# One layer of a hybrid network on one core: where the second doubled block of weights stands, and how a norm's scale reaches all partitions

## The chip, the cores and the metric

The kernel runs on one core of one Trainium2 chip. The metric is the device time of one launch in microseconds (us); lower is better. Three runs of the kernel before gave 2309.09 us in the median (2308.48 to 2310.07).

## The reference

One layer works on 256 tokens of 2048 features, all in fp32:

```python
h = h + 0.5 * swiglu(rmsnorm(h, ffn1_norm), ffn1_w_in, ffn1_w_out)          # 2048 -> 2 x 5632 -> 2048
h = h + hybrid_mixer(rmsnorm(h, mix_norm), ...)                             # 2048 -> 11296, 4096 -> 2048
h = h + 0.5 * swiglu(rmsnorm(h, ffn2_norm), ffn2_w_in, ffn2_w_out)
gate = sigmoid(rmsnorm(h, ple_norm) @ ple_w_gate)
h = h + gate * (p @ ple_w_proj)
return rmsnorm(h, final_norm)
# rmsnorm(x, w) = x * rsqrt(mean(x * x, features) + 1e-6) * w
```

The mixer holds a short gated convolution, a state-space part over two chunks of 128 tokens and 32 heads (each product with its own decay mask), and a norm over four groups of 512 features. So a token's mean square over 2048 features is wanted five times and over 512 features four times: nine norms.

## The kernel before

Features lie on the 128 partitions, tokens along the free axis: `h` is 128 x 16 x 256. Every large product is a `Gemm` object. It takes 256 output columns (two halves `j` of 128, a PSUM bank each) and walks the depth in chunks of four 128-row tiles. For each chunk SyncE loads 512 KB of weights (`w`, four buffers), ScalarE rounds them to `hi` (line 99) and VectorE makes `lo = w - hi` (line 100); `hi` and `lo` have three buffers each. The input is likewise held as a high part (columns 0 to 255) and a low part (256 to 511). Each depth tile then costs a pair of products: H (`hi` against 512 columns) and L (`lo` against the 256 high columns). Line 136 issues both. The results are added when the gemm ends (`gather`: ScalarE line 150, VectorE line 152).

In a chunk and half the four pairs stand as HLHLHLHL, or as HHLLHHLL, which I call a double block. Which ones do is set by `doubles`, line 120: the number is `k0 % 16 // 2 + j`, from 0 to 7 over four chunks with two halves each. The default (0, 4) gives two double blocks in every 32 pairs, twelve ordinary pairs apart; in the two feed-forward parts (`ffn`) only one number is given, so 24 to 32 ordinary pairs lie between.

A norm (class `Norm`) sums squares per partition into `nacc` (128 x 256). `sums` multiplies it, once per 128 tokens, as the stationary operand with one column of ones (line 194), so that the sums of 256 tokens stand on partitions as 128 x 2. VectorE scales and adds epsilon (line 211), GpSimd takes the power -0.5 of these two columns (line 213). `spread` brings this back to all partitions, with two products against the identity (line 221) and a copy to SBUF (line 224). Eight norms go this way; the last one has a variant for the end of the kernel. As a norm's factor multiplies the result of the product that follows, `sums` is called one gemm ahead of `spread`, and that gemm runs meanwhile.

The engines get their instructions from a scheduling layer that fixes an order for each engine; every engine works its queue strictly in that order. The weights' `hi` and `lo` have a raised priority (line 98).

Of the kernel before, what the change touches and what calls it, by code (L numbers as in the profile page):

```python
# [8 lines left out]
F32 = mybir.dt.float32  # L9
F32R = mybir.dt.float32r  # L10
AF = mybir.ActivationFunctionType
ALU = mybir.AluOpType
PSUM = bass.MemoryType.PSUM

P = 128
T = 256
D = 2048
KD = D // P
# [5 lines left out]
NCH = 2  # L24
EPS = 1e-6
KC = 4
# [19 lines left out]
S_ALL = S_CB + 24  # L46


@with_exitstack
def block_kernel(ctx, tc, xT, pT, small, dtp, w1, o1, wm, wdt, om, w2, o2, wg, wp, out):  # L50
    nc = tc.nc
    cst = ctx.enter_context(tc.tile_pool(name="cst", bufs=1))
# [3 lines left out]
    ev = ctx.enter_context(tc.tile_pool(name="ev", bufs=2))  # L56
    tmp = ctx.enter_context(tc.tile_pool(name="tmp", bufs=1))
# [5 lines left out]
    def aux(name):  # L63
        return aux_p.tile([P, 512], F32, tag="aux", name=name)
# [21 lines left out]
    V.tensor_scalar(out=mneg, in0=stri, scalar1=NEG, scalar2=None, op0=ALU.mult)  # L86
    pick = cst.tile([2 * HEADS, HEADS], F32R, name="pick")
    V.tensor_tensor(out=pick, in0=ident[0:2 * HEADS, 0:HEADS], in1=ident[0:2 * HEADS, HEADS:2 * HEADS], op=ALU.add)
    half = cst.tile([P, 2], F32, name="half")
    G.memset(half, -0.5)  # L90


    def parts(src, nk, cols):
# [10 lines left out]
    class Gemm:  # L104
# [2 lines left out]

        def __init__(self, src, K, rhs, cols=256, one=False, acc=None, doubles=(0, 4)):  # L110
            self.src, self.K, self.rhs, self.cols, self.one, self.doubles = src, K, rhs, cols, one, doubles
            self.acc = acc_p.tile([P, 2, 512], F32, tag="acc", name="acc") if acc is None else None
            self.banks = [self.acc[:, j, :] for j in range(2)] if acc is None else acc

        def chunk(self, k0, k1):
            hi, lo = parts(self.src[:, k0:k1, :], k1 - k0, self.cols)
            for j in range(self.cols // P):
                js = slice(j * P, (j + 1) * P)
                order = "HL" * (k1 - k0)
                if k1 - k0 == KC and k0 % 16 // 2 + j in self.doubles:  # L120
                    order = "HHLLHHLL"
                todo, acc, nh, nl = [], self.banks[j], k0, k0
                for part in order:
                    if part == "H":
                        k, w, nh = nh, hi, nh + 1
                    else:
                        k, w, nl = nl, lo, nl + 1
                    x, a = self.rhs(k), w[:, k - k0, js]
                    if self.one:
                        todo += [(acc[:, 0:T], a, x[:, i:i + T]) for i in ((0, T) if part == "H" else (0,))]  # L130
                    elif part == "H":
                        todo.append((acc, a, x))
                    else:
                        todo.append((acc[:, T:], a, x[:, 0:T]))
                for n, (o, a, b) in enumerate(todo):
                    nc.tensor.matmul(o, lhsT=a, rhs=b, start=(k0 == 0 and n == 0),  # L136
                                     stop=(k1 == self.K and n == len(todo) - 1))
# [6 lines left out]
    def gemm(*args, **kw):  # L144
        return Gemm(*args, **kw).all()
# [28 lines left out]
    class Norm:  # L174
# [24 lines left out]
            self.total(self.acc, self.ps, True, False)  # L199

        def sums(self):
            v = tmp.tile([P, 2], F32, tag="nv", name="nv", bufs=2)
            if self.more is None:
                ps = aux("nps")
                self.total(self.acc, [ps[:, c:c + 1] for c in range(NCH)], True, True)
                src = [(v, ps[:, 0:2])]
            else:
                self.total(self.more[:, 0, :], self.ps, False, True)
                src = [(v[:, c:c + 1], self.ps[c]) for c in range(NCH)]
            for o, i in src:  # L210
                V.tensor_scalar(out=o, in0=i, scalar1=1.0 / self.n, scalar2=EPS, op0=ALU.mult, op1=ALU.add)
            rt = tmp.tile([P, 2], F32, tag="nrt", name="nrt", bufs=2)
            G.tensor_tensor(out=rt, in0=v, in1=half, op=ALU.pow)  # L213
            self.rt = rt

        def spread(self, both=False):
            rt = self.rt
            pbs = [aux("npb") for _ in range(2 if both else 1)]
            for pb in pbs:
                for c in range(NCH):  # L220
                    nc.tensor.matmul(pb[:, c * P:(c + 1) * P], lhsT=rt[:, c:c + 1].to_broadcast([P, P]),  # L221
                                     rhs=ident, start=True, stop=True)
            r = tmp.tile([P, T], F32, tag=self.tag, name="r", bufs=2)
            (A.copy if both else V.tensor_copy)(out=r, in_=pbs[-1][:, 0:T])
            return (pbs[0], r) if both else r

        def finish(self, both=False):
            self.sums()
            return self.spread(both)

    def next_x(src, m, x, wcol, norm):

# [6 lines left out]
    def ffn(wi, wo, x, norm, wcol_next, begun=()):  # L239
        xn, nn, r = None, Norm(D, "rn"), None  # L240
        f0 = 0
        for third, nf in enumerate((15, 15, 14)):
            ga = blk.tile([P, 8, 512], F32R, tag="blk", name="ga")
            gb = blk.tile([P, 8, 512], F32R, tag="blk", name="gb")
            gx = lambda k: (ga if k < 8 else gb)[:, k % 8, :]
            held = []
            for f in range(nf):
                acc = begun[f].acc if f0 + f < len(begun) else gemm(wi[f0 + f], KD, x, doubles=(f % 2,))
                held.append((f, gather(acc)))
                if r is None and f == 0:  # L250
                    if not begun:
                        norm.sums()
                    continue
                if r is None:
                    r = norm.spread()
                for i, s in held:
                    V.tensor_tensor(out=s, in0=s, in1=bc2(r), op=ALU.mult)
                    sg = ev.tile([P, T], F32, tag="t1", bufs=5, name="sg")
                    A.activation(out=sg, in_=s[:, 0, :], func=AF.Silu)
                    V.tensor_tensor(out=sg, in0=sg, in1=s[:, 1, :], op=ALU.mult)  # L260
                    split(gx(i), sg)
                held = []
            if third == 2:
                xn = new_x()
            for m in range(0, KD, 2):
                acc = gemm(wo[m // 2][:, f0:f0 + nf, :], nf, gx, doubles=(0,))
                s = gather(acc, scale=0.5)
                hm = h[:, m:m + 2, :]
                V.tensor_tensor(out=hm, in0=s, in1=hm, op=ALU.add)
                if third == 2:  # L270
                    next_x(hm, m, xn, wcol_next, nn)
            f0 += nf
        return xn, nn
# [272 lines left out]
    for m in range(0, KD, 2):  # L546
        tail = m == KD - 2
        pr = proj(m) if tail else None
        for q in range(2 if tail else 1):
# [22 lines left out]
            for i in range(m + q, m + q + n):  # L572
                if i < POOL:
                    A.activation(out=hw[:, i, :], in_=h[:, i, :], func=AF.Copy,
                                 scale=sm[:, S_NF + i:S_NF + i + 1])
    pb, rf = nf.finish(both=True)
    for i in range(POOL):
        G.tensor_tensor(out=hw[:, i, :], in0=hw[:, i, :], in1=rf, op=ALU.mult)
        if i in (1, POOL - 1):
# [70 lines left out]
```

## Time and profile before

| | |
|---|---|
| median of three runs | 2309.09 us |
| the profiled execution | 2308.93 us, span 2307.2 us |
| TensorE busy | 2289.1 us (99%), 13308 products |
| VectorE, ScalarE busy | 1510.6 us (65%), 1140.1 us (49%) |
| GpSimd busy | 11.8 us (1%), 25 instructions |
| granted TensorE clock | 0.998 of full speed in the mean |

TensorE is busy in nearly all slices of the span, but matmuls overlap in the trace, so that "busy" doesn't say how dense they stand. The distance from one start to the next does, and it is what the rows below show.

### The profile page before, as it was taken

What the parts mean: (1) busy time and instruction counts of PE and PEld (TensorE: products, weight loads), DVE (VectorE), ACT (ScalarE), POOL (GpSimd) and SP (SyncE); (2) the same over time, 40 slices, a digit from 0 to 9 for tenths busy, and PEclk for the clock granted to TensorE, in tenths of its full rate; (3) what the DMA queues carried; (4) which work ended last, traced back from release to release, by engine and by line L of the source; (5) the groups of instructions that cost most, each with busy time, mean ns of one, the idle gap of its engine ahead of it and who ended that gap; (6) DMA issues with size and microseconds to landing.
All of it is one profiled execution on the core that took longest, in us unless ns stands there. A gap on an engine that the chain in (4) does not pass through costs nothing.

```text
span 2307.2 us, 33578 instructions
## 1 busy us (share of the span) xinstructions
PE 2289.1 (99%) x13308; PEld 1995.2 (86%) x13308; DVE 1510.6 (65%) x1936; ACT 1140.1 (49%) x1499; POOL 11.8 (1%) x25
## 2 busy tenths in 40 slices
PE   8999999999999999999999999999999999999997
PEld 7888888888888888888888888888888888888887
DVE  7665566656667777777777655566656665666776
ACT  6444444444455555444455444444444444444564
POOL 0000000000000000000000000000000000000000
PEclk9999999999999999999999999999999999999999
DMA  7666666665666655555555666666666666666654
GB/s 240 190 189 184 195 191 189 186 193 190 191 183 194 187 186 183 164 164 173 172 175 182 180 190 184 186 189 191 189 191 189 190 190 187 192 190 183 193 183 143
DMA packets 126862, 429.38 MB, mean 186 GB/s; under 512 B 13616, under 2 KB 20016, under 8 KB 126704
## 3 DMA queue, kind: packets, MB, share of 16 engines
q1 hardware_dynamic: 126144, 426.17, 61.1%
q8 instruction: 104, 1.70, 0.3%
q10 hardware_dynamic: 480, 0.80, 0.1%
q14 instruction: 54, 0.44, 0.0%
q0 software_dynamic: 80, 0.26, 0.0%
HBM read 425.08 MB, written 2.10 MB: 185 GB/s over the span
## 4 chain that ended last, share of the span: by engine, by line
PE 99%; DVE 0%; DMA 0%; ACT 0%; POOL 0%; issue 0%; DVEq 0%; POOLq 0%; ACTq 0%
PE acc L136 97%; PE pr L136 0%; PE yp L417 0%; PE ab L398 0%; PE npb L221 0%; DVE h L583 0%; DMA sm<-in_small 0%; PE yp L420 0%; PE xt L373 0%; PE st L387 0%; PE nps L194 0%; PE cb L366 0%; DVE xa L163 0%; POOL nrt L213 0%; PE dtT L432 0%
## 5 line engine op out<-in xcount | busy, mean ns | idle before, releaser
L100 DVE TENSOR_TENSOR lo<-w,hi 128x1024 fp32r<-128x1024 f32 (+1 forms) x834 | 990.6, 1188 | 703.6 <-ACT hi L99 690.2
L99 ACT CAST hi<-w 128x1024 fp32r<-128x1024 f32 (+1 forms) x834 | 850.9, 1020 | 1019.5 <-PE acc L136 835.2
L136 PE MATMUL acc<-xb,hi 128*128 128x512 f32 (+1 forms) x2264 | 782.1, 393 | 0.0
L136 PE MATMUL acc<-xa,hi 128*128 128x512 f32 (+1 forms) x2264 | 774.4, 395 | 6.1 <-DVE xa L163 6.1
L136 PE MATMUL acc<-xb,lo 128*128 128x256 f32 x2248 | 606.6, 278 | 0.0
L136 PE MATMUL acc<-xa,lo 128*128 128x256 f32 x2248 | 580.7, 279 | 0.0
L136 PEld LDWEIGHTS acc<-xb,hi 128*128 128x128 f32 x2264 | 415.7, 188 | 89.1 <-issue 0.7
L136 PEld LDWEIGHTS acc<-xa,hi 128*128 128x128 f32 x2264 | 405.0, 188 | 80.1 <-ACT hi L99 6.1
L136 PEld LDWEIGHTS acc<-xa,lo 128*128 128x128 f32 x2248 | 423.3, 188 | 25.7 <-DVE lo L100 0.7
L136 PEld LDWEIGHTS acc<-xb,lo 128*128 128x128 f32 x2248 | 422.2, 188 | 10.2 <-issue 0.5
L136 PE MATMUL acc<-ga,hi 128*128 128x512 f32 x768 | 262.3, 394 | 0.0
L136 PE MATMUL acc<-gb,hi 128*128 128x512 f32 x640 | 224.2, 394 | 0.0
L136 PE MATMUL acc<-ga,lo 128*128 128x256 f32 x768 | 197.3, 277 | 0.0
L136 PE MATMUL acc<-gb,lo 128*128 128x256 f32 x640 | 177.3, 277 | 0.0
L136 PEld LDWEIGHTS acc<-ga,hi 128*128 128x128 f32 x768 | 137.2, 188 | 25.1
L136 PEld LDWEIGHTS acc<-ga,lo 128*128 128x128 f32 x768 | 144.2, 188 | 8.5
L136 PEld LDWEIGHTS acc<-gb,hi 128*128 128x128 f32 x640 | 120.0, 188 | 27.9
L152 DVE SCALAR_TENSOR_TENSOR esum<-acc,elo 128x512 f32<-128x512 f32 (+1 forms) x196 | 133.6, 681 | 0.0
L136 PEld LDWEIGHTS acc<-gb,lo 128*128 128x128 f32 x640 | 120.1, 188 | 0.0
L150 ACT ACTIVATE elo<-acc 128x512 f32<-128x512 f32 (+1 forms) x196 | 116.1, 592 | 0.0
L136 PE MATMUL acc<-yb,hi 128*128 128x512 f32 x256 | 88.4, 398 | 0.0
L136 PE MATMUL acc<-ya,hi 128*128 128x512 f32 x256 | 88.3, 398 | 0.0
(144 smaller groups left out, 1108.9 us busy)
## 6 DMA issues: line engine op xcount, KB each, us to landing
w<-in_w SPq DMA_DIRECT2D x350, 512.0 KB, 4.5
w<-in_wm SPq DMA_DIRECT2D x176, 512.0 KB, 3.8
w<-in_o SPq DMA_DIRECT2D x144, 512.0 KB, 3.7
w<-in_om SPq DMA_DIRECT2D x64, 512.0 KB, 3.6
w<-in_wg SPq DMA_DIRECT2D x28, 512.0 KB, 4.5
w<-in_o SPq DMA_DIRECT2D x32, 384.0 KB, 3.7
w<-in_o SPq DMA_DIRECT2D x16, 256.0 KB, 3.4
w<-in_wp SPq DMA_DIRECT2D x8, 256.0 KB, 2.6
```

The lines of the kernel that those rows point to most:

```text
L99: A.copy(out=hi[:, :nk, :cols], in_=w[:, :nk, :cols])
L100: V.tensor_tensor(out=lo[:, :nk, :cols], in0=w[:, :nk, :cols], in1=hi[:, :nk, :cols].bitcast(F32), op=ALU.subtract)
L136: nc.tensor.matmul(o, lhsT=a, rhs=b, start=(k0 == 0 and n == 0), stop=(k1 == self.K and n == len(todo) - 1))
L150: A.mul(out=lo[:, :n, :], in_=acc[:, :n, T:], mul=scale)
L152: V.scalar_tensor_tensor(out=s[:, :n, :], in0=acc[:, :n, 0:T], scalar=scale, in1=lo[:, :n, :], op0=ALU.mult, op1=ALU.add)
```

## The change

Two things. The double blocks: `doubles` becomes `orders`, a table from the same number to an order. Number 0 keeps HHLLHHLL; number 1 ends in a double half and number 2 begins with one, so that the second block of four doubled pairs lies over the border of two halves and begins two ordinary pairs behind the first block, and 22 ordinary pairs follow. The feed-forward calls name one number as before and keep their order.

The norms: a matrix filled with 1/n is the stationary operand of one product whose moving operand is `nacc` (256 columns). Its result is the mean on every partition. VectorE adds epsilon over 256 columns, GpSimd takes the power over 256 columns into `r`, and the two products against the identity and the copy are gone. The last norm keeps its way.

```diff
+TWICE = {0: "HHLLHHLL", 1: "HLHLHHLL", 2: "HHLLHLHL"}
...
-    half = cst.tile([P, 2], F32, name="half")
+    half = cst.tile([P, T], F32, name="half")
     G.memset(half, -0.5)
+    mean = {}
+    for w in (D, 512):
+        mean[w] = cst.tile([P, P], F32, name=f"mean{w}")
+        G.memset(mean[w], 1.0 / w)
...
-                if k1 - k0 == KC and k0 % 16 // 2 + j in self.doubles:
-                    order = "HHLLHHLL"
+                if k1 - k0 == KC:
+                    order = self.orders.get(k0 % 16 // 2 + j, order)
...
         def sums(self):
...
+            ps = aux("nps")
+            nc.tensor.matmul(ps[:, 0:T], lhsT=mean[self.n], rhs=self.acc, start=True, stop=True)
+            v = ev.tile([P, T], F32, tag="t1", bufs=5, name="nv")
+            V.tensor_scalar(out=v, in0=ps[:, 0:T], scalar1=EPS, scalar2=None, op0=ALU.add)
+            self.r = tmp.tile([P, T], F32, tag=self.tag, name="r", bufs=2)
+            G.tensor_tensor(out=self.r, in0=v, in1=half, op=ALU.pow)
+
+        def spread(self):
+            return self.r
...
-                acc = begun[f].acc if f0 + f < len(begun) else gemm(wi[f0 + f], KD, x, doubles=(f % 2,))
+                acc = begun[f].acc if f0 + f < len(begun) else gemm(wi[f0 + f], KD, x, orders={f % 2: TWICE[0]})
...
-                acc = gemm(wo[m // 2][:, f0:f0 + nf, :], nf, gx, doubles=(0,))
+                acc = gemm(wo[m // 2][:, f0:f0 + nf, :], nf, gx, orders={0: TWICE[0]})
...
-    pb, rf = nf.finish(both=True)
+    pb, rf = nf.last()
```

TensorE at the first group norm of the mixer. Before, the two column sums, then one double block and ordinary pairs:

```order
L194 MATMUL nps<-ones,nacc 128x1 x2
L136 MATMUL acc<-xa,hi 128x512 x2
L136 MATMUL acc<-xa,lo 128x256 x2
L136 MATMUL acc<-xa,hi 128x512 x2
L136 MATMUL acc<-xa,lo 128x256 x2
L136 MATMUL acc<-xa,hi 128x512
L136 MATMUL acc<-xa,lo 128x256
L136 MATMUL acc<-xa,hi 128x512
L136 MATMUL acc<-xa,lo 128x256
```

Now, at the same place (`mean_106` is the matrix of 1/512):

```order
L211 MATMUL nps<-nacc,mean_106 128x256
L143 MATMUL acc<-xa,hi 128x512 x2
L143 MATMUL acc<-xa,lo 128x256 x2
L143 MATMUL acc<-xa,hi 128x512 x2
L143 MATMUL acc<-xa,lo 128x256 x2
L143 MATMUL acc<-xa,hi 128x512
L143 MATMUL acc<-xa,lo 128x256
L143 MATMUL acc<-xa,hi 128x512
L143 MATMUL acc<-xa,lo 128x256
L143 MATMUL acc<-xa,hi 128x512 x2
L143 MATMUL acc<-xa,lo 128x256 x2
L143 MATMUL acc<-xa,hi 128x512 x2
```

One product stands in place of two, and the second double block has come up from twelve pairs behind the first to two.

VectorE behind the same norm's line 211. Before (`nv` is the row ahead of these), the copy of `r` and the products with it (`yn`) stand some ten instructions on, one gemm later:

```order
L100 TENSOR_TENSOR lo<-w,hi 128x1024
L152 SCALAR_TENSOR_TENSOR esum<-acc,elo 128x512
L502 TENSOR_TENSOR esum<-esum,r 128x512
L100 TENSOR_TENSOR lo<-w,hi 128x1024
L504 TENSOR_TENSOR XT<-XT,esum 128x512
L100 TENSOR_TENSOR lo<-w,hi 128x1024
L187 TENSOR_TENSOR nacc<-sq 128x256
L100 TENSOR_TENSOR lo<-w,hi 128x1024
L224 COPY r<-npb 128x256
L100 TENSOR_TENSOR lo<-w,hi 128x1024
L152 SCALAR_TENSOR_TENSOR esum<-acc,elo 128x512
L487 SCALAR_TENSOR_TENSOR yn<-XT,sm,r 128x256 x4
```

Now:

```order
L213 TENSOR_SCALAR nv<-nps 128x256
L107 TENSOR_TENSOR lo<-w,hi 128x1024
L159 SCALAR_TENSOR_TENSOR esum<-acc,elo 128x512
L494 SCALAR_TENSOR_TENSOR yn<-XT,sm,r 128x256
L509 TENSOR_TENSOR esum<-esum,r 128x512
L494 SCALAR_TENSOR_TENSOR yn<-XT,sm,r 128x256
L107 TENSOR_TENSOR lo<-w,hi 128x1024
L511 TENSOR_TENSOR XT<-XT,esum 128x512
```

The first user of GpSimd's power (`yn`) has moved up to the third place behind `nv`, with one `lo` and one `esum` between; the next `lo` now stands behind it. (The `r` of line 509 is an older one.)

## Rows read from the trace of the kernel before

**Rows 1.** The page, part 4: the chain that ended last, by engine.

```profile
PE 99%; DVE 0%; DMA 0%; ACT 0%; POOL 0%; issue 0%; DVEq 0%; POOLq 0%; ACTq 0%
```

**Rows 2.** Busy time by stretch: length, PE, PEld, DVE, ACT, POOL, clock, DMA.

```profile
80.00:750.00 670.00, 670.00 (x3865) 585.64 (x3864) 418.97 (x484) 323.95 (x414) 0.00 (x0) 1.00 0.63 190
1290.18:1459.18 169.00, 169.00 (x963) 146.77 (x961) 94.95 (x110) 77.38 (x93) 0.00 (x0) 1.00 0.64 186
```

**Rows 3.** Timeline, PE, in the first feed-forward part: start us, us, engine, line.

```profile
303.31 0.39 PE L136 MATMUL acc<-xb,hi 128*128 128x512 f32 x1
...
304.00 0.39 PE L136 MATMUL acc<-xb,hi 128*128 128x512 f32 x1
```

**Rows 4.** Timeline, PE, in the mixer's output product.

```profile
1352.14 0.40 PE L136 MATMUL acc<-ya,hi 128*128 128x512 f32 x1
...
1352.49 0.40 PE L136 MATMUL acc<-ya,hi 128*128 128x512 f32 x1
...
1352.86 0.40 PE L136 MATMUL acc<-ya,hi 128*128 128x512 f32 x1
...
1353.20 0.40 PE L136 MATMUL acc<-ya,hi 128*128 128x512 f32 x1
```

**Rows 5.** Timeline, PE: the first and the last long pair.

```profile
33.92 0.40 PE L136 MATMUL acc<-xa,hi 128*128 128x512 f32 x1
...
34.28 0.40 PE L136 MATMUL acc<-xa,hi 128*128 128x512 f32 x1
...
2210.34 0.40 PE L136 MATMUL acc<-xa,hi 128*128 128x512 f32 x1
...
2210.70 0.62 PE L136 MATMUL acc<-xb,hi 128*128 128x512 f32 x2
```

**Rows 6.** Busy time by stretch: the twelve pairs on either side of that double block.

```profile
2206.46:2210.70 4.24, 4.24 (x26) 3.67 (x25) 3.25 (x4) 2.71 (x3) 0.00 (x0) 1.00 0.66 207
2212.09:2216.25 4.16, 4.16 (x26) 3.63 (x25) 2.14 (x4) 2.38 (x4) 0.00 (x0) 1.00 0.67 219
```

**Rows 7.** Timeline, PE: a group norm's two pairs of products and what follows them.

```profile
1217.79 0.50 PE L194 MATMUL nps<-ones,nacc 128*128 128x1 f32 x4
1218.15 0.72 PE L136 MATMUL acc<-xa,hi 128*128 128x512 f32 x2
...
1219.64 0.40 PE L136 MATMUL acc<-xa,hi 128*128 128x512 f32 x1
...
1229.51 0.60 PE L221 MATMUL npb<-ident,nrt 128*128 128x128 f32 x4
1229.88 0.71 PE L136 MATMUL acc<-xa,hi 128*128 128x512 f32 x2
```

**Rows 8.** Timeline, PE: a plain fp32 product with 512 moving columns.

```profile
926.93 1.02 PE L387 MATMUL st<-xe,CB 128*128 128x512 f32 x2
927.88 0.73 PE L398 MATMUL ab<-sums,pick 64*128 64x256 f32 x4
```

**Rows 9.** Timeline, DVE, at the group norm of rows 7.

```profile
1218.40 0.16 DVE L211 TENSOR_SCALAR nv<-nps 128x2 f32<-128x2 f32 x1 [0.95 <-PE nps L194]
...
1220.13 0.69 DVE L152 SCALAR_TENSOR_TENSOR esum<-acc,elo 128x512 f32<-128x512 f32 x1
...
1222.22 1.23 DVE L100 TENSOR_TENSOR lo<-w,hi 128x1024 fp32r<-128x1024 f32 x1 [0.67 <-ACT hi L99]
...
1230.16 0.42 DVE L224 COPY r<-npb 128x256 f32<-128x256 f32 x1 [1.04 <-PE npb L221]
...
1232.47 1.66 DVE L487 SCALAR_TENSOR_TENSOR yn<-XT,sm,r 128x256 f32<-128x256 f32 x4
```

**Rows 10.** Timeline, PE: the fourth chunk of the gemm that begins at 1218.15.

```profile
1226.68 0.40 PE L136 MATMUL acc<-xb,hi 128*128 128x512 f32 x1
```

**Rows 11.** Groups of instructions on POOL: busy us, mean ns.

```profile
L213 POOL TENSOR_TENSOR nrt<-nv,half 128x2 f32<-128x2 f32 x9 | 6.3, 695 | 1892.9 <-DVE nv L211 1892.9
L578 POOL TENSOR_TENSOR hw<-hw,r 128x256 f32<-128x256 f32 x5 | 3.5, 731 | 1.7 <-ACT r L224 1.7
```

More of the change, by code (lines that the diff above doesn't have):

```diff
@@ L104, in block_kernel, with __init__ @@
     class Gemm:
-        def __init__(self, src, K, rhs, cols=256, one=False, acc=None, doubles=(0, 4)):
-            self.src, self.K, self.rhs, self.cols, self.one, self.doubles = src, K, rhs, cols, one, doubles
+        def __init__(self, src, K, rhs, cols=256, one=False, acc=None, orders=TWICE):
+            self.src, self.K, self.rhs, self.cols, self.one, self.orders = src, K, rhs, cols, one, orders
             self.acc = acc_p.tile([P, 2, 512], F32, tag="acc", name="acc") if acc is None else None
@@ L201, in sums, with last @@
         def sums(self):
[L202 to L218, printed above, removed]
+            ps = aux("nps")
[6 more added lines that the diff above has]
+            return self.r
+        def last(self):
+            self.total(self.more[:, 0, :], self.ps, False, True)
+            v = tmp.tile([P, 2], F32, tag="nv2", name="nv2")
+            for c in range(NCH):
+                V.tensor_scalar(out=v[:, c:c + 1], in0=self.ps[c], scalar1=1.0 / self.n, scalar2=EPS,
+                                op0=ALU.mult, op1=ALU.add)
+            rt = tmp.tile([P, 2], F32, tag="nrt", name="nrt")
+            G.tensor_tensor(out=rt, in0=v, in1=half[:, 0:2], op=ALU.pow)
+            pbs = [aux("npb") for _ in range(2)]
             for pb in pbs:
@@ L223, in spread @@
             r = tmp.tile([P, T], F32, tag=self.tag, name="r", bufs=2)
[L224 to L229, printed above, removed]
+            A.copy(out=r, in_=pbs[1][:, 0:T])
+            return pbs[0], r
     def next_x(src, m, x, wcol, norm):
```

## The prediction

> **What bounds the kernel now.** I began with the chain of waits: 99% of the span is TensorE [rows 1]. So no wait of another engine matters unless it reaches TensorE, and the question is how densely its products stand. The busy share can't say that, so I took the busy time by stretch, for its counts. Two products make a pair. In the first feed-forward part 3865 products fill 670.00 us, 346.7 ns a pair; in the mixer's output product 960 of the 963 counted (three overlap the border) fill 169.00 us, 352.1 ns a pair [rows 2]. The clock is 1.00 in both and the shapes are the same, so the difference lies in the order.
>
> The timeline shows its form, if only the starts of the H products are read. In the feed-forward part two pairs take 0.69 us [rows 3], again and again. In the output product the pairs run in threes: 0.35, 0.37 and 0.34, together 1.06 us [rows 4], where three at the former pace would take 1.04. I call these the rhythm of two and the rhythm of three; the latter costs 0.020 us in every three pairs. Its mark is a long pair, the second of the three, with a start-to-start of 0.36 us or more, whose H alone takes about 240 ns. Going through the whole timeline I counted 321 such pairs, from 33.92 to 2210.34 us [rows 5]: 136 between 884 and 1218 (the state-space part, where small products cut into the stream), 25 between 1218 and 1289 (group norms), 129 from there to 1469 (the output product), 31 elsewhere. All of it is 321 x 0.020 = 6.4 us.
>
> What ends the rhythm of three? The last long pair shows it: a double block begins right behind the second pair of a three, and the twelve pairs ahead of it took 4.24 us, the twelve behind it 4.16 [rows 5, 6]. Where the block begins behind the third pair, the next three starts over at the block's end: that is every block of the output product, since twelve ordinary pairs are four whole threes [rows 4]. Small products and waits in between throw the stream back into it. In the rhythm of two a double block on an even count leaves that rhythm as it is, as in all of rows 3's stretch.
>
> **The change, part by part.** *Double blocks.* The number of doubled pairs is the same, 8 in 32. What moves is the second four: two pairs behind the first, then 22 ordinary ones. If the first block leaves the stream in threes, one starts at its end, and two pairs on the second block stands behind the second pair, which is the place that healed in rows 5 and 6. If the first block has healed it, 2 and 22 are even and it stays so. So the rhythm of three should last from an interruption to the second block behind it. By the order, the output product keeps about 4 long pairs of 129, the group norms 4 of 25. In the state-space part small products cut into the stream five times for each of the four groups, and by the order 1 to 16 ordinary pairs follow a cut before the next block; I count about 16 long pairs that remain in each group, 64 of 136. The two feed-forward parts keep their order, and a run of 24 or 32 pairs must end at the right place by itself: I put 28 there. With 10 for the rest about 110 remain, and 211 x 0.020 = 4.2 us go. The ends: 0 (nothing heals) and 6.4 (everything); a loss is excluded as every count behind a block is even.
>
> *The norm's products.* Of a norm before, the column sums hold the stream from 1217.79 to 1218.15, 0.36 us, and the double block behind takes 1.49 us where it takes 1.39 undisturbed (four pairs at 346.7 ns), 0.10 more; the products against the identity take 0.37, and the block behind begins alike, 0.10 more [rows 7]. Together 0.93. The new product, 128 x 256 in plain fp32, isn't in the trace. The nearest is the 128 x 512 one in two passes, 0.95 us to the next product [rows 8]; half the columns give 0.475, plus 0.10 for the block behind, 0.575. That saves 0.355, for eight norms 2.8 us. The ends: at the whole price of rows 8, 0.12 is lost on each, 1 us in all; at the price of the column sums (0.46) 3.8 us are gained. I take 2.8.
>
> *VectorE.* `nv` grows from 0.16 us to what a copy of 256 columns out of PSUM takes, 0.42, and that copy goes [rows 9]. The sum is -0.16 us a norm, beside a busy TensorE: nothing. Three fills at the start on GpSimd stand before anything that waits for them: nothing.
>
> *The power over 256 columns.* Here lies the risk. Two columns take 695 ns; 256 columns of a plain product on the same engine take 731 [rows 11]. Its lower end is therefore 0.73 us, since it does no less. Its upper end is 128 times 695 ns, 89 us. The order puts the first user of `r` on VectorE only one `lo` and one `esum` behind `nv`, and VectorE stands still there until GpSimd is done; behind it wait an `esum` (0.69), two `yn` (0.42 each by rows 9) and then the `lo` for the gemm's fourth chunk, 1.23 us. TensorE starts that chunk 1226.68 - 1217.79 = 8.9 us after the norm's products [rows 7, 9, 10]. So `r` must be there 8.9 - 1.23 - 1.5 = 6.2 us after the product starts; product, hand-over (0.61 from its start to `nv` before) and `nv` take 1.1 of these, with 0.1 for the start on GpSimd, which leaves 5.0 us for the power. I reckon the same for all eight norms, though one or two stand tighter. I take 3.6 us, near the plain product, which has the same shape: the 695 ns are mostly start, and the columns cost four times the 2.9 ns that a column of the plain product costs at most (0.7 + 254 x 0.0114). Then it is hidden: TensorE works on chunks whose `lo` is ready.
>
> **Sum**, against the profiled execution's 2308.93 us: 2308.93 - 4.2 - 2.8 = 2301.9 us. The median of the runs is 0.2 higher, so the same number stands for it.
>
> **Rivals.**
>
> *The power is late.* From 5.0 us on every further us holds VectorE, then TensorE, eight times. At 5.9 us the 7.0 us are used up, at 6.5 the kernel is slower by more than 0.2%. For it speaks that two columns already take 695 ns, about as long as 256 columns of a product: if most of that is work and not start, each column costs up to 350 ns. Against it: the rows have no third width, so a start of 0.6 us explains them as well. Between 5.0 and 89 us the middle by ratio is 21 us: 2301.9 + 8 x 16 = 2430 us; at the upper end 2301.9 + 8 x 84 = 2974. The wait would also be a gap in TensorE's stream, behind which its clock could fall from the level of 1.00; I add nothing for it. A rule for this one: the Trainium skill (GPSIMD Engine Reference, Performance pitfalls for Q7 kernels) says that a chain of fp32 steps that wait for each other costs 4 cycles per element for each step, unless several elements are worked on side by side. By that rule the root's price grows with every column, as at the upper end; no row here shows which it is.
>
> *The order is worth nothing.* Then only the norms' 2.8 us are gained: 2306.1. It would be so if the new product leaves TensorE in a condition from which the two blocks don't heal, or if the second block, which lies over a border between two halves and waits for nothing, behaves otherwise than one inside a half. Rows 5 and 6 speak against it. The Trainium skill (TensorE: Matmul & The Clock Gate, Back-to-back issue gap) states a gap of N/2.4 ns + 2.5 for warm products, 325 ns for a pair of 512 and 256 columns in any order. By that the double blocks' place could not matter; the trace disagrees, with 346.7 and 352.1 ns for one and the same pair.
>
> **How the numbers follow.** The runs before agree within 0.07%; about 0.2% (4.6 us) is what a measurement of this kernel can tell from no change. The forecast has a chance of 0.50, with its own range from 2298.5 to 2304.5; the order worth nothing 0.10; a power of 5.0 to 6.5 us, which ends within 0.2%, 0.04; a later one 0.36. Faster by over 0.2% (below 2304.5) is 0.50, as the forecast's upper edge lies there; same 0.14; slower 0.36. For the range, 0.64 lies up to 2313.7. Of the late case I take in what lies up to a power of 17 us, a little under half of it by ratio, which brings the sum near 0.8: 2301.9 + 8 x 12 = 2398. So 2298 to 2398.
>
> **What would show it.** Right: in the output product the busy time by stretch gives 347 ns a pair instead of 352.1; between 1218 and 1289 the threes vanish behind each second double block; GpSimd's row for the power is below 5 us, and VectorE's wait for it doesn't show up as idle time of TensorE. The product at line 211 should hold the stream some 0.5 us. Wrong: TensorE idle with VectorE's `lo` as the releaser a few us behind each line 211; or threes that go on behind the second block; or a power of tens of us, where all else is lost in its price.

## The result and the profile after

The kernel after takes 2610.66 us (median of three, 2610.49 to 2611.57) against 2309.09, a ratio of 1.1306 [1.1291, 1.1322]. Forecast were 2301.9 us and at most 2398. The rival "The power is late" came true, at a price beyond the range. Of 50 executions of the kernel before in the two later series, 7 lie between 2305.73 and 2306.85 us and 43 between 2308.30 and 2310.48, at the same granted clock (0.997 to 0.998); the profiled one (2308.93 us) is like the 43.

The page first: part 1 (busy time), three rows of the slices, and the chain by engine, which answers to [rows 1].

```profile
span 2608.9 us, 33479 instructions
...
PE 2301.8 (88%) x13260; PEld 2004.2 (77%) x13260; DVE 1512.1 (58%) x1928; ACT 1141.3 (44%) x1499; POOL 336.8 (13%) x27
...
PE   4899999999994999999933369949999999999948
...
POOL 5100000000006000000166720060000000000150
PEclk8899999999997999999976679979999999999979
...
PE 85%; POOL 13%; DVE 1%; ACT 0%; issue 0%; DMA 0%; POOLq 0%; ACTq 0%
```

TensorE has holes exactly where GpSimd is busy, and GpSimd holds 13% of a chain in which it had 0%. The group that answers to [rows 11] says why (busy us, mean ns, idle before):

```profile
L215 POOL TENSOR_TENSOR r<-nv,half 128x256 f32<-128x256 f32 x8 | 330.0, 41251 | 1785.4 <-DVE nv L213 1785.4
```

One power over 256 columns takes 41.25 us; I had put 3.6 there and a cover of 5.0. How it reaches TensorE is read at one group norm, which answers to [rows 7, 9, 10]. VectorE's timeline (start, length, and in brackets the idle time before with what ended it):

```profile
1296.26 0.42 DVE L213 TENSOR_SCALAR nv<-nps 128x256 f32<-128x256 f32 x1 [0.97 <-PE nps L211]
1296.84 1.75 DVE L107 TENSOR_TENSOR lo<-w,hi 128x1024 fp32r<-128x1024 f32 x1 [0.15 <-ACT hi L106]
1298.51 0.68 DVE L159 SCALAR_TENSOR_TENSOR esum<-acc,elo 128x512 f32<-128x512 f32 x1
1338.08 0.48 DVE L494 SCALAR_TENSOR_TENSOR yn<-XT,sm,r 128x256 f32<-128x256 f32 x1 [38.89 <-POOL r L215]
...
1339.48 1.22 DVE L107 TENSOR_TENSOR lo<-w,hi 128x1024 fp32r<-128x1024 f32 x1
```

After one `lo` and one `esum` the first user of `r` stands at the head of VectorE's queue and waits 38.89 us; the next chunk's `lo` waits behind it. TensorE's timeline at the same place:

```profile
1295.63 0.59 PE L211 MATMUL nps<-nacc,mean 128*128 128x256 f32 x2
1295.87 0.82 PE L143 MATMUL acc<-xa,hi 128*128 128x512 f32 x2
...
1304.41 0.40 PE L143 MATMUL acc<-xb,hi 128*128 128x512 f32 x1
1340.75 0.58 PE L143 MATMUL acc<-xb,lo 128*128 128x256 f32 x1 [35.95 <-DVE lo L107]
1341.13 0.63 PE L143 MATMUL acc<-xb,hi 128*128 128x512 f32 x1
1341.56 0.41 PE L143 MATMUL acc<-xb,lo 128*128 128x256 f32 x1
1341.77 0.63 PE L143 MATMUL acc<-xb,hi 128*128 128x512 f32 x1
```

It works on for 8.8 us from the norm's product to its last start (8.9 were reckoned), and then stands. Behind the gap an H lasts 0.43 us from start to start (1341.13 to 1341.56) and an L 0.21, against 0.23 and 0.12 undisturbed: the lower level of the clock, 1.2 GHz instead of 2.4. Busy time by stretch over the first norm's gap and just behind it shows the grant (the number before the last two):

```profile
40.00:74.00 34.00, 0.00 (x0) 0.00 (x0) 1.48 (x2) 0.76 (x2) 32.48 (x1) 0.53 0.00 0
74.00:84.00 10.00, 9.60 (x42) 8.32 (x43) 7.23 (x11) 5.26 (x8) 0.00 (x0) 0.74 0.64 192
```

TensorE's waits in sum (us in total, times, longest):

```profile
PE acc L143 <- DVE lo L107: 285.7, 8, 37.1
...
PE acc L143 <- ACT hi L106: 3.7, 4, 0.9
```

The account, counted from start to start in the trace after: eight gaps of 34.1 to 37.5 us, 287 us beyond the normal distance; 9 to 19 products at the lower clock behind each, 18.2 us; four new waits on `hi` in the state-space part, 4.4 us; long pairs 77 instead of 321, -4.9 us; the norms' products, -4.0 us (below). Together 300.7; measured 301.6. (A long pair is counted where an H takes 238 to 246 ns to the L behind it.)

### The profile page after: what moved, and what is told of

The parts are those of the page before. It is cut to its first block, busy times and chain, and to the rows that moved or that the text cites. A ratio compares the mean times of both kernels' runs of the same rounds, so it can differ in the third digit from the quotient of the medians.

```text
span 2608.9 us, 33479 instructions
## 1 busy us (share of the span) xinstructions
PE 2301.8 (88%) x13260; PEld 2004.2 (77%) x13260; DVE 1512.1 (58%) x1928; ACT 1141.3 (44%) x1499; POOL 336.8 (13%) x27
## 4 chain that ended last, share of the span: by engine, by line
PE 85%; POOL 13%; DVE 1%; ACT 0%; issue 0%; DMA 0%; POOLq 0%; ACTq 0%
PE acc L143 84%; POOL r L215 13%; DVE lo L107 0%; PE pr L143 0%; PE yp L424 0%; PE ab L405 0%; ACT hi L106 0%; DMA sm<-in_small 0%; ACT L L416 0%; PE xt L380 0%; PE yp L427 0%; PE st L394 0%; DVE nv L213 0%; POOL hw L585 0%; PE nps L211 0%
## 5 line engine op out<-in xcount | busy, mean ns | idle before, releaser
L143 PE MATMUL acc<-xb,lo 128*128 128x256 f32 x2248 | 632.5, 281 | 248.6 <-DVE lo L107 248.6
L143 PE MATMUL acc<-xb,hi 128*128 128x512 f32 (+1 forms) x2264 | 800.3, 397 | 0.0
L143 PEld LDWEIGHTS acc<-xb,lo 128*128 128x128 f32 x2248 | 429.3, 191 | 252.3 <-DVE lo L107 250.8
L143 PE MATMUL acc<-xa,lo 128*128 128x256 f32 x2248 | 562.9, 278 | 0.0
L215 POOL TENSOR_TENSOR r<-nv,half 128x256 f32<-128x256 f32 x8 | 330.0, 41251 | 1785.4 <-DVE nv L213 1785.4
L143 PEld LDWEIGHTS acc<-xb,hi 128*128 128x128 f32 x2264 | 430.0, 190 | 98.6
L143 PEld LDWEIGHTS acc<-xa,hi 128*128 128x128 f32 x2264 | 398.7, 189 | 76.1 <-ACT hi L106 11.2
L264 DVE TENSOR_TENSOR esum<-esum,r 128x512 f32<-128x512 f32 x88 | 61.0, 693 | 82.7 <-POOL r L215 79.7
```

The costliest lines, as they stand in the source:

```text
L215: G.tensor_tensor(out=self.r, in0=v, in1=half, op=ALU.pow)
```

## The experiments

Ratios are against the kernel before on the same chip in the same series; its median was 2306.85, 2309.25 and 2309.17 us in the three series, so times of different series aren't set side by side without it. The 27 executions of the first series (2306.05 to 2307.95 us) are nearer to the 7 above than to the 43; e1 to e4 belong to it.

**Which half of the change costs.** Two kernels, each with one part of the change alone: the blocks in the kernel before, and the kernel after with the old blocks.

```diff
 # e1_blocks_only: before, and
+TWICE = {0: "HHLLHHLL", 1: "HLHLHHLL", 2: "HHLLHLHL"}
 # e2_norms_only: after, and
-TWICE = {0: "HHLLHHLL", 1: "HLHLHHLL", 2: "HHLLHLHL"}
+TWICE = {0: "HHLLHHLL", 4: "HHLLHHLL"}
```

> Only the double blocks move (second one two pairs behind the first); the norms are as before. Theory: the 301 us are the norms' alone, and the blocks heal the rhythm of three: long pairs (H start to start of 238 to 246 ns) fall from 321 to about 80, which is 4.8 us. Against it stand four new waits of about 1.1 us that the changed kernel shows in the state-space part (a PE start to start of 1.34 us at 1038, 1114, 1189 and 1265 us), because the instructions' order there changed with the blocks: 2308.9 - 4.8 + 4.4, about 2308.5 us. Rival (blocks worth nothing or harmful by themselves): 321 long pairs stay and the time is 2309 to 2314. If the four waits belong to the norms instead, it is 2304.

> Only the norms change (one product, power over 256 columns); the double blocks stand twelve pairs apart as before. Theory: eight powers of 41.2 us, each holding TensorE about 36 us and then costing about 2.3 us at the lower clock level: 2309 + 8 x 38 - 3 = 2610 us, give or take 3. Rival (the two edits only cost together, through the order of instructions): clearly less than 2600.

Measured: the norms alone 2613.49 us, 1.1330 [1.1309, 1.1351]; the blocks alone 2309.57, 1.0010 [1.0001, 1.0019]. The loss is the norms' (2607 to 2613 us were expected). The blocks did to the rhythm what was forecast: against the profiled execution of the kernel before, 109 long pairs of 321 are left (2 of 129 in the output product, 3 of 25 at the group norms, 48 of 136 in the state-space part, elsewhere 56 where there were 31), -4.2 us. Yet nothing was gained. Among TensorE's waits in that trace is:

```profile
...
PE acc L139 <- ACT hi L102: 3.7, 4, 0.9
```

This row isn't among the waits of the kernel before. One of the four, on TensorE:

```profile
1039.75 0.40 PE L139 MATMUL acc<-xb,hi 128*128 128x512 f32 x1
1041.04 0.50 PE L139 MATMUL acc<-xa,hi 128*128 128x512 f32 x1 [0.89 <-ACT hi L102]
1041.37 0.28 PE L139 MATMUL acc<-xb,lo 128*128 128x256 f32 x1
```

and on ScalarE:

```profile
1039.00 1.06 ACT L412 ACTIVATE L<-L 128x1024 f32<-128x1024 f32 x1
1039.95 1.04 ACT L102 CAST hi<-w 128x1024 fp32r<-128x1024 f32 x1
```

An H of the next product (`xa`) has been put ahead of the rest of this one's last half (`xb`), and its `hi` is still being made, as ScalarE had the decay masks first. In the kernel before the `xb` products and the small ones behind them come first there. 1.29 us from start to start instead of 0.23, and 1.29 to 1.34 at the four: +4.3 us. That makes +0.1 against the profiled execution, and 2309.57 lies 0.6 above it. The +2.7 [0.2, 4.4] against this series is for the most part a difference on the other side: the kernel before ran some 2 us shorter in it. What such a difference can come from is seen in the next run.

**The power off the path.** The kernel before with powers of several widths whose result nobody uses.

```diff
+    extra = [[(256, ALU.pow)],
+             [(128, ALU.pow), (64, ALU.pow), (32, ALU.pow), (8, ALU.pow), (2, ALU.pow), (256, ALU.mult), (2, ALU.mult)],
+             [(256, ALU.pow)]]
...
+                G.tensor_tensor(out=pw[:, 0:w], in0=r[:, 0:w], in1=half[:, 0:w], op=op)
```

> The kernel before, with extra powers on GpSimd that nobody waits for: 256 columns behind the first and the seventh norm, and behind the second norm 128, 64, 32, 8 and 2 columns, then a plain product of 256 and of 2 columns. Theory (price per column): 0.38 us + 0.160 us a column, so 20.8, 10.6, 5.5, 1.7 and 0.70 us, and 41.2 for 256; time as before, 2309 within 2 us, since only the wait costs. Rival (GpSimd's work itself holds the memory ports that VectorE shares): VectorE's lo instructions of 1.22 us get longer while a power runs, and the kernel is slower by more than 5 us. Second rival (price by steps or with a large start): 128 columns and 256 differ by less than 1.5 in ratio.

Measured: 2306.97 us, 1.0004 [0.9995, 1.0013]. A power of 41 us costs nothing that shows when nobody waits for it:

```profile
1479.75 41.24 POOL L231 TENSOR_TENSOR pw<-r,half 128x256 f32<-128x256 f32 x1 [11.15 <-DVE r L228]
```

VectorE's `lo` beside the powers keeps its median of 1.225 us. Only the `lo` that begins together with a wide power is longer: 1.80 us here (and 1.63 beside the plain product of 256 columns), 1.75 to 1.81 at six powers of the kernel after, 1.34 to 1.41 with powers of 128 columns, where none of the 762 in the kernel before takes over 1.3. That is half a us at a norm, so contention is out as the cause of the loss. The groups on GpSimd give the price by width:

```profile
L231 POOL TENSOR_TENSOR pw<-r,half 128x128 f32<-128x128 f32 x1 | 21.8, 21824 | 11.4 <-DVE r L228 11.4
L231 POOL TENSOR_TENSOR pw<-r,half 128x64 f32<-128x64 f32 x1 | 10.5, 10547 | 0.1
L217 POOL TENSOR_TENSOR nrt<-nv,half 128x2 f32<-128x2 f32 x9 | 6.3, 699 | 1794.6 <-DVE nv L215 1794.6
L231 POOL TENSOR_TENSOR pw<-r,half 128x32 f32<-128x32 f32 x1 | 5.4, 5431 | 0.1
...
L231 POOL TENSOR_TENSOR pw<-r,half 128x8 f32<-128x8 f32 x1 | 1.6, 1636 | 0.1
```

It is nearly a straight line: 0.16 us a column, and about 0.38 us of start. Of the 0.70 us of two columns nearly half was work. (The extra power of two columns took 2.04 us here, three times as long as `nrt`, and the one of 128 columns 21.8 where it takes 20.8 in e9; off the path, with VectorE at work beside them, three of the powers lie 0.9 to 1.3 us higher. The trace doesn't show why.) The Trainium skill (GPSIMD Engine Reference, Performance pitfalls for Q7 kernels) says that a chain of dependent fp32 steps is paid for each element; the trace agrees in form, as the price grows with every column, and shows no number of steps.

This run shows something else besides. Its double blocks stand as before, yet its trace has 169 long pairs and none of them in the output product. The same stretch in e3 and in the kernel before:

```profile
1296.00:1458.00 162.00, 162.00 (x936) 141.56 (x935) 90.91 (x100) 74.20 (x88) 0.00 (x0) 1.00 0.66 190
1296.00:1458.00 162.00, 162.00 (x921) 140.67 (x921) 89.66 (x99) 72.78 (x86) 0.00 (x0) 1.00 0.64 188
```

With the old blocks the output product keeps whichever rhythm it is entered with. The 152 long pairs fewer are 3.0 us (the profiled executions differ by 2.3), about what parts the two groups of times of the kernel before. That the rhythm is what parts those too is argued, not shown: no trace shows one of its short executions.

**The blocks side by side.** Numbers 0 and 1 instead of 0 and 4, norms of before.

```diff
+TWICE = {0: "HHLLHHLL", 1: "HHLLHHLL"}
```

> The kernel before with the second double block directly behind the first (numbers 0 and 1), 24 ordinary pairs behind. Theory: a block that begins behind a whole three leaves the rhythm of three as it was, so the first block and the second both start over a three, 24 pairs are eight whole threes, and the output product keeps its 352 ns a pair: about 120 long pairs there, time 2309 within 1.5 us. Rival (what counts is only that the blocks stand close together): the output product falls to 347 ns a pair and about 2.4 us go.

Measured: 2311.78 us, 1.0021 [1.0012, 1.0030]. The output product kept 1 long pair of 129; it runs at 347.1 ns a pair (925 products, three of them over the border):

```profile
1300.00:1460.00 160.00, 160.00 (x925) 139.82 (x924) 90.05 (x99) 73.42 (x86) 0.00 (x0) 1.00 0.66 190
```

That looks as if a block right behind another healed too, but the trace shows otherwise. The output product was entered in twos: behind the first blocks, at 1293.62 us, 24 pairs follow without a long one. Where 24 pairs in threes did run into the two blocks, eight times between 946 and 1212 us, the 24 pairs behind were in threes all eight times. At the last of them (an H of 0.24 us to its L is a long pair's):

```profile
1210.90 0.40 PE L139 MATMUL acc<-xb,hi 128*128 128x512 f32 x1
1211.14 0.28 PE L139 MATMUL acc<-xb,lo 128*128 128x256 f32 x1
...
1211.61 0.63 PE L139 MATMUL acc<-xa,hi 128*128 128x512 f32 x2
...
1214.75 0.40 PE L139 MATMUL acc<-xa,hi 128*128 128x512 f32 x1
1214.99 0.28 PE L139 MATMUL acc<-xa,lo 128*128 128x256 f32 x1
```

So the rule held: behind a whole three a block changes nothing (in the kernel before at 52 of 52 places). Behind the second pair of a three it ends the threes: 6 of 6 in the kernel before, 15 of 16 in e1, whose output product was entered in threes and healed at its second block. 178 long pairs remain in e4 (-2.9 us), and the waits on `hi` come up here as well (four of 1.28 us, +4.2). That is +1.3 against the profiled execution of the kernel before, and 2311.78 lies 2.9 above it; of the other 1.5 us the trace gave no account.

**Another root.** The kernel after with a square root on ScalarE, from PSUM, and a reciprocal on VectorE in the power's place; and with that, the blocks close together (e5) or apart as before (e11).

```diff
...
-            V.tensor_scalar(out=v, in0=ps[:, 0:T], scalar1=EPS, scalar2=None, op0=ALU.add)
+            A.activation(out=v, in_=ps[:, 0:T], func=AF.Sqrt, bias=epst)
...
-            G.tensor_tensor(out=self.r, in0=v, in1=half, op=ALU.pow)
+            V.reciprocal(out=self.r, in_=v)
```

> The kernel after with one edit: the power over 256 columns on GpSimd is replaced by a square root on ScalarE, which reads the mean out of PSUM and adds eps, and a reciprocal over 256 columns on VectorE; products and double blocks stay as in the kernel after. Theory (what was lost is the 41.25 us of GpSimd's power, less the cover of about 5 us, eight times, and the clock behind each gap): a reciprocal over 256 columns takes 1.74 us on VectorE before (32 partitions, line 347), a table load on ScalarE 1.28 us, so r is there about 3.5 us after the mean, within the cover. All 287 us of gaps and the 18 us of the lower clock go: the time of the blocks alone (1.0010 of before) less the 2.8 us of the cheaper products, a ratio of 0.999 to 1.001. Rival (the new form of the norm itself holds TensorE, whoever takes the root): half or more of the loss stays, a ratio above 1.05. Second rival (two table loads for each of eight norms come into the way of `hi`): 8 x 2.6 = 21 us, a ratio of 1.008 to 1.010.

> The norm of the kernel after with its root on ScalarE and VectorE, and all double blocks at 0 and 4 as before: the norm's products alone, with a root that is hidden. Theory (prediction's term: 0.93 us become 0.575 at each of eight norms): 2.8 us less than before, a ratio of 0.9985 to 0.999. Rival (the state that the new product leaves throws the stream into the rhythm of three: 520 long pairs were counted with the kernel after's norms and old blocks, 199 more than before, 4.0 us): the gain is eaten up, a ratio of 1.000 to 1.001.

Measured: e5 2305.74 us, 0.9983 [0.9974, 0.9992], a little below the expected 0.999 to 1.001: the whole loss goes with the power, and the form of the norm is free of blame. At one norm, ScalarE's and then VectorE's timeline:

```profile
1285.18 1.05 ACT L108 CAST hi<-w 128x1024 fp32r<-128x1024 f32 x1 [1.19 <-issue]
1286.24 1.28 ACT L215 ACT_TABLE_LOAD   x1
1287.54 0.47 ACT L215 ACTIVATE nv<-nps,epst 128x256 f32<-128x256 f32 x1
```

```profile
1288.05 1.75 DVE L217 RECIPROCAL r<-nv 128x256 f32<-128x256 f32 x1 [0.56 <-ACT nv L215]
1289.78 1.23 DVE L109 TENSOR_TENSOR lo<-w,hi 128x1024 fp32r<-128x1024 f32 x1
```

From the table load to `r` are 3.6 us, within the cover. The Trainium skill (ScalarE: Activation LUTs, What ACT_TABLE_LOAD costs) gives 1283 ns for the load and about 1380 ns of drain on top. The load agrees; no such drain shows here, as the `hi` cast, the load and the root follow each other without a gap. The tables' second rival (20 us) is out.

e11 took 2309.16 us, 1.0001 [0.9992, 1.0009], against an expected 0.9985 to 0.999; its rival held. 535 long pairs were counted, 214 more than before, 4.3 us: 90 instead of 8 between 748 and 884 us, 60 instead of 4 from 2200 us on. That eats what the new product's shortness saves. It isn't that the new product alone leaves the stream in threes: in the kernel before threes follow the column sums as well (behind the block at 754.27 us), but the products against the identity cut in a gemm later, and behind them (from 765.98) the pairs run in twos; so it is at three of the group norms. The new norm has no second cut, and in e11 the threes run on from the block at 753.37 us to 884. With a second block close behind, which ends them, the products pay (e5, e8).

**The user put back.** The kernel after with the first user of `r` tied to the next product's result, at seven norms.

```diff
+            V.scalar_tensor_tensor(out=self.r, in0=done[-1][:, 0, :], scalar=0.0, in1=self.r,
+                                   op0=ALU.mult, op1=ALU.add)
```

> The kernel after with one edit: at seven of the eight norms the first user of r on VectorE stands behind the work of the next product on VectorE (a tie to the next product's gathered result), the power stays 41.25 us on GpSimd. Theory (the gap of TensorE is the power less the work that VectorE and TensorE still have in hand when the user of r comes): a product lasts 11.1 us, so seven gaps of about 36 us become about 25: 2610.7 - 7 x 11 = 2533 us, 2520 to 2550. Rival (TensorE is held by GpSimd itself, by its traffic on PSUM or SBUF, and not through VectorE's order): the gaps stay, 2600 to 2615 us.

Measured: 2567.56 us, 1.1117 [1.1097, 1.1137], 43 us less than after where 77 were expected. Of the seven gaps, from start to start, three shrank by 9 to 10 us (to 25.5, 25.8 and 27.5), two by 6 (to 30.0) and one by 1.9; the one at the output product's end stayed, with a second wait of 2.2 us behind it. The gap depends on the place of the user, so VectorE's order is how the power reaches TensorE, but the seven places give less room than I took.

**Narrower powers on the path.** The kernel after with the power over 128 or 32 of the columns; the other columns of `r` get a constant, so the kernel leaves that part of the computation out.

```diff
+            V.tensor_scalar(out=self.r[:, 0:c], in0=ps[:, 0:c], scalar1=EPS, scalar2=None, op0=ALU.add)
+            V.tensor_scalar(out=self.r[:, c:T], in0=ps[:, c:T], scalar1=0.0, scalar2=0.05, op0=ALU.mult, op1=ALU.add)
+            G.tensor_tensor(out=self.r[:, 0:c], in0=self.r[:, 0:c], in1=half[:, 0:c], op=ALU.pow)
```

> The kernel after, but the power of the eight norms runs over the first 128 of the 256 columns; the others of r get the constant 0.05, so this part of the computation is left out. GpSimd took 21.82 us for 128 columns off the path. Theory (TensorE loses the power less a cover of 5.0 us, eight times, and the clock behind each gap): the time with a hidden root, 0.9983 x 2309.1 = 2305.2, plus 8 x (21.8 - 5.0) = 134.6, plus 14 to 18 for the clock: 2454 to 2458 us, gaps of about 16.5 us. Rival (the cover isn't a constant: with a shorter power other work fills more of it): under 2430 us. Rival (a price of the form of the norm, whatever the width): above 2550 us.

> As the kernel with the power over 128 columns, with 32 columns instead (the other 224 of r get a constant and are left out of the computation). GpSimd took 5.43 us for 32 columns off the path, just above the cover of 5.0 us that the prediction reckoned. Theory: gaps of TensorE of 0.2 to 0.6 us at most at each norm, 2305.2 + 8 x 0.43 = 2308.6 us, a ratio of 0.999 to 1.001, and no clock to pay. Rival (any wait of VectorE on GpSimd costs TensorE a stretch at the lower clock, or the cover is well under 5 us): 2320 us or more, a ratio above 1.004.

Measured: 2449.12 us, 1.0606 [1.0587, 1.0626], and 2309.50, 1.0003 [0.9994, 1.0012]. The first lies 5 us under the expected range, as its power takes 20.8 us where 21.8 were reckoned. At 128 columns (20.8 us) TensorE loses 15.3 us in the mean from start to start; at 256 it is 41.25 and 35.9.

```profile
L216 POOL TENSOR_TENSOR r<-r,half 128x128 f32<-128x128 f32 x8 | 166.3, 20787 | 1784.4 <-DVE r L214 1784.4
PE acc L143 <- DVE lo L107: 121.2, 8, 16.9
```

What is hidden is 5.5 and 5.4 us: a constant, near my 5.0. At 32 columns the waits of TensorE on `lo` are nearly gone:

```profile
L216 POOL TENSOR_TENSOR r<-r,half 128x32 f32<-128x32 f32 x8 | 43.5, 5436 | 1771.7 <-DVE r L214 1771.7
```

```profile
PE acc L143 <- DVE lo L107: 2.0, 2, 1.4
```

The lower clock cost about 19 us in all behind gaps of 13.5 to 17.3 us and 18 behind those of 34 to 37; behind the gaps of 0.9 to 1.8 us of the 32 columns, and behind the waits on `hi` of 1.29 to 1.34 us, the products ran at the higher level again at once.

**Blocks only where they pay.** e12 is the kernel before with the blocks close together outside the first feed-forward products and the state-space loop; e7 the same with the norm and root of e5; e8 is e7 with the first gate product, which follows the loop, left as before too (the diff's last two lines).

```diff
+APART = {0: "HHLLHHLL", 4: "HHLLHHLL"}
...
-            s = mix_pair(n)
+            s = mix_pair(n, APART)
...
-            s = mix_pair(n)
+            s = mix_pair(n, APART if j == 0 else TWICE)
```

> The kernel before with the second block two pairs behind the first in the mixer's first twelve products, the gates under the group norms, the output product and the output head only; the first two feed-forward products and the state-space part's loop keep blocks at 0 and 4; norms as before. Theory (with the blocks alone the rhythm gained 4 us and four new waits of 1.1 us in the state-space part gave it back): the waits don't come up, the output product keeps at most 4 long pairs of 129 (2.5 us), the gates a few of 25: 2.5 to 3.5 us less than before, a ratio of 0.9985 to 0.999. Rival (the loss comes from the blocks wherever they stand, by entries into the rhythm of three elsewhere): 1.000 to 1.001, as with the blocks alone.

> The kernel before run as e5 with its root on ScalarE and VectorE, but the double blocks stay at 0 and 4 of 8 in the first two feed-forward products and in the state-space part's loop over eight, and stand close together only in the other products (mixer's first twelve, gates under the group norms, output product, output head). Theory: no new waits in the state-space part, so the loss of about 4.5 us that the blocks alone bring there goes, the output product's gain of 2.6 us and the gates' 0.4 stay, and the norm's products give 2.8: about 5 us less than before, a ratio of 0.997 to 0.999. Rival (table loads on ScalarE cost what the products save, or more): 1.000 or above. If the blocks' loss isn't the new order in the state-space loop, the ratio equals that of e5.

> The kernel with the root on ScalarE and mixed blocks (0.9978 of before), with the blocks of the first gate product, the one that follows the state-space loop, at 0 and 4 again as well. In that run one of the four waits on `hi`, 1.34 us at 1187.49, was left, and the product behind the loop had its blocks close together. Theory (the wait comes up where the product that follows state-space work has its blocks close together): the wait goes, 1.1 us less, a ratio of 0.997 to 0.998. Rival (the wait comes from the norm's other instructions): it stays, with the ratio at 0.9978.

Measured: e12 2307.40 us, 0.9993 [0.9984, 1.0002], which can't be told from no change where 0.9985 to 0.999 was expected; its trace has 150 long pairs (-3.4 us) and one wait of the four (+1.1), so -2.3, near the -1.85 of the medians. e7 2304.16 us, 0.9978 [0.9969, 0.9987], with the same single wait, at 1187.49, where the gates follow the loop. e8 2302.67 us, 0.9971 [0.9961, 0.9982]: there TensorE's waits are these, with no `hi` among them:

```profile
PE acc L146 <- DVE xa L173: 6.2, 1, 6.2
PE nps L204 <- ACT sq L192: 2.0, 1, 2.0
PE npb L235 <- POOL nrt L231: 1.1, 1, 1.1
```

So the wait comes up where the product that follows state-space work has its blocks close together. e8 beats both kernels: its seven executions (2302.12 to 2303.18 us) lie below all of the kernel before. Its output product and a group norm answer to [rows 2] and [rows 7]:

```profile
1296.00:1458.00 162.00, 162.00 (x935) 141.60 (x934) 92.32 (x103) 75.84 (x90) 0.00 (x0) 1.00 0.66 191
```

```profile
1217.35 0.59 PE L214 MATMUL nps<-nacc,mean 128*128 128x256 f32 x2
1217.59 0.82 PE L146 MATMUL acc<-xa,hi 128*128 128x512 f32 x2
...
1219.17 0.40 PE L146 MATMUL acc<-xa,hi 128*128 128x512 f32 x1
```

935 products in 162 us, two of them over the border, are 347.3 ns a pair, where it was 352.1. The norm's product holds the stream for 0.24 us and the block behind takes 1.58 instead of 1.39.

## Why the prediction was wrong

- **The power over 256 columns.** This is the step that failed: "I take 3.6 us, near the plain product, which has the same shape: the 695 ns are mostly start". It measures 41.25 us. Both ends of the bound were named, 0.73 and 89 us, and I chose by the row of like shape (a product of 256 columns) instead of the row of like operation (a power of two columns). The start is 0.38 of the 0.70 us, so 0.16 us a column.
- **The cover** was right: 5.0 us reckoned, 5.4 to 5.5 measured (e9). The rival's own formula with the true power, 2301.9 + 8 x (41.25 - 5.0), gives 2592 us.
- **The clock**: "I add nothing for it". It was 18 us, and with it the formula gives 2610. That this meets 2610.66 so closely is luck in part: the gaps were 3 us shorter than the formula has them and the two small gains 1.9 us larger, and the four new waits took 4.4 back.
- **The double blocks**: 109 long pairs left with the blocks alone, forecast about 110, -4.2 us as forecast. The rule behind it held (e4), but that the count agrees is luck in part: forecast were 4, 4, 64 and 38 for output product, group norms, state-space part and the rest, and 2, 3, 48 and 56 were left. And 4.2 us is the gain over an execution like the profiled one; e3's trace has no threes in the output product with the blocks as before. (The 346.7 ns a pair of the feed-forward part counts two products over the border, which the 352.1 leaves out; by starts it is 346.9.) What I missed is that the new table also changes the order in which the scheduler sets the state-space part: four waits of 1.1 us, shown to go with the blocks by e1 (all four) and e8 (the last of them). So a loss wasn't "excluded", as the prediction has it. I had looked at the order there for the pairs behind each cut, and not for whether each H's `hi` is made in time.
- **The norm's products**: 0.93 us become 0.24 + 0.19 = 0.43, not 0.575, so 4.0 us instead of 2.8. That they alone gain nothing, as no second cut ends the threes behind them any more (e11), wasn't foreseen.
- "The order is worth nothing" is wrong for the output product (2 long pairs left in e1) and came out near the truth for the whole of e1, for another reason than I gave. The formula that this rival cites from the Trainium skill (TensorE: Matmul & The Clock Gate, Back-to-back issue gap) is given there for a product by itself, so the two paces of a stream neither bear it out nor refute it.
- Of the signs named for "wrong", TensorE idle with VectorE's `lo` as the releaser came up, but 8.8 us behind the product.

What stays open: some 1.5 us of e4 that neither long pairs nor waits account for, and what decides, with the blocks as before, whether the output product is entered in twos or in threes.

## What to carry to other kernels

When an unknown cost has bounds 100 times apart, choose the row of the same operation over the row of the same shape, and price the end that hurts with its consequences (here the clock). Before a function goes from two columns to 256 on GpSimd, have a second width; a root that waits at the head of VectorE's queue needs an engine that does it within the cover, here ScalarE and VectorE in 3.6 us. A change of order made for one stage is best kept to that stage, and the new order is to be read for operands that aren't ready, not only for what it heals. Before a difference of 2 or 3 us is put down to an edit, see whether the kernel it is measured against has such a difference in itself, and count the rhythm in both traces.

## What the runs showed of the hardware

- A power on GpSimd: 0.70, 1.64, 5.43, 10.55, 20.8 to 21.8 and 41.25 us for 2, 8, 32, 64, 128 and 256 columns on 128 partitions; a product of 256 columns 0.73.
- A `lo` on VectorE that begins together with such a power of 256 columns takes 1.75 to 1.81 us instead of 1.22, and 1.34 to 1.41 with 128 columns; those that begin later in it keep 1.22 (e3).
- The two rhythms of the same pairs, 347 and 352 ns, last for hundreds of pairs. A double block behind a whole three left the threes as they were at 52 of 52 places (kernel before); one behind the second pair of a three ended them at 6 of 6 there and at 15 of 16 in e1.
- A reciprocal of 256 columns takes 1.75 us on VectorE on 128 partitions, and the same on 32.
- TensorE's loss to the lower clock was 1.4 to 2.9 us behind each gap, whether the gap lasted 13.5 or 37 us; gaps up to 1.8 us brought none.
- A plain fp32 product of 256 columns holds the stream for 0.24 us and the H behind it for 0.42 instead of 0.23.
